# Second product of the feed-forward block as seven products on quarters, in a two-layer hybrid block on one core

## The chip, the cores and the metric

One core of a Trainium2 chip runs the whole program. The metric is device time in microseconds of one execution, the median of several. All arithmetic is fp32: TensorE multiplies a rounded type (fp32r), so a product of two fp32 matrices is made of three matmuls (below).

## What is computed

Two layers over 512 tokens of 1024 numbers, weights of each layer different:

```python
def reference(x, positions, ...):
    for l in range(2):
        h = rms_norm(x, pre_mix_norm[l])
        z = h @ w_in[l]                       # 1024 -> 1932, split in 13
        mix = concat(conv_group(..), pool_group(..), sgu_group(..), nsa_group(..))
        x = x + rms_norm(mix @ w_out[l], post_mix_norm[l])
        h = rms_norm(x, pre_ffn_norm[l])
        f = square(relu(h @ ffn_w1[l]))       # 512x1024 @ 1024x4096
        x = x + rms_norm(f @ ffn_w2[l], post_ffn_norm[l])   # 512x4096 @ 4096x1024
    return x
```

The change is in the last two lines of the loop, the feed-forward block (ffn), and in where some tiles of the four mixers lie.

## The kernel before

**One recorder orders everything.** The program first records every instruction of the five engines in `_Rec.add`, with what it depends on, an assumed duration (`cost`) and a key: its place in the recording plus `shift`. `order` then takes, again and again, the engine that can start an instruction earliest by these assumed durations, and on it the instruction that is ready first, ties by key; tiles of a pool are handed out in recorded order. `issue` writes the result out, so the order on each engine is fixed, and each instruction waits for semaphores only. All instructions come out of `issue`, which is why every row of the profile shows line L442; tiles tell them apart. Transfers go into the assumed time as one stream (L401 to L406): bytes at 360 per ns, then 2 us for one of SyncE and 4 for one of GpSimd.

**Products.** An fp32 operand is split in hi and lo parts: ScalarE copies it, rounding (`wh` of a weight tile `wr`), and VectorE subtracts (`wl`). `mm3` (L473) multiplies hi by hi, hi by lo, lo by hi into one PSUM bank. A weight tile (a unit, 128x1024, 512 KB) is loaded by SyncE into one of six `wr` buffers and split into one of five places for `wh` and `wl`. A sum of weight tiles is made by a transfer on GpSimd's queue that adds another tile of memory to the buffer (`more`).

**First product of the ffn.** The 4096 inner columns are taken in four parts of 1024; each part in two halves `i` of 512. `square4` does a half by seven products on quarters (Winograd's form of Strassen's scheme): the tokens, the inner rows and the columns are halved; the seven left forms (`hF`: A11, A12, A22, S1 to S4) are built from the normed input by `norm_forms` once per layer, and the right ones come from four weight tiles by adding transfers. Its PSUM banks are named `pf`. The results are squared after ReLU and split into the tiles `f` (hi and lo, 512 columns for every row tile of 128 inner columns).

**Second product of the ffn.** It is a plain product, per part 8 row tiles of `f` by 4 token tiles, for each of two halves of 512 output columns: `tgroup` runs over units of two row tiles, with three 512-column matmuls a pair. The left half of the columns goes to `pm` banks and is summed over the parts in `y` (ScalarE copies in part 0, VectorE adds later); the right half keeps four own banks `po` over all parts. In the last part VectorE and ScalarE also make the squares and the products with the gain `gb`, `post` adds to `xres`, and `norm_tile` builds `h` and its transpose `hT` for the next layer, one token tile after another.

**Memory.** Twelve tiles of 8 KB per partition (`big`) hold `hF`, `f`, `y`, mixer outputs and weights ahead; gains lie in a small pool (`grow`), and the mixers' convolution inputs `ch`, `V`, `Vc`, `pch` and `cst` in the pool `mp`.

PSUM has eight banks, three under the tag "mm", one "o", two "s", two "x"; the `po` banks take "x" and "s" for the whole ffn. What this section calls the last first product of a part is the last use of a `pf` bank in it.

## Time and profile before

| | |
|---|---|
| median of 3 runs | 1082.05 us (1081.45 to 1082.11) |
| profiled execution | 1081.48 us, its span 1079.8 us |
| TensorE busy in the span | 1064.2 us (99%) |
| VectorE busy | 726.2 us (67%) |
| ScalarE busy | 505.8 us (47%) |
| GpSimd busy | 92.7 us (9%) |
| granted TensorE clock, mean | 0.998 |

The busy times are shares of one span in which different stages alternate: the mixers, the output product, four ffn parts, twice. A part is 84 us, so the eight parts make 672 us of it. Which engine sets the end of a stage is to be read from that stage: windows show each engine's busy time in a stretch, the chain of waits shows what released what, and the timeline shows single instructions.

### The profile page before, as it was taken

The page shows a single profiled execution, that of the slowest core. Times are in us where ns is not written, and L with a number is a line of the kernel's source. Part 1 is how long each engine was busy: PE and PEld are TensorE (multiplying, and loading weights), DVE is VectorE, ACT ScalarE, POOL GpSimd, SP SyncE. Part 2 cuts the span into 40 slices and gives each one's busy share as a digit, 9 for nine tenths or more (in the row PEclk, how much of TensorE's full clock was granted, in tenths as well). Part 3 has the DMA queues.
Part 4 walks back from the last instruction along what each step waited for, and adds up shares of the span by engine and source line. Part 5 has one row for each costly group of instructions (what it writes and reads, how often), then busy time and mean ns, then how long its engine had stood idle before and what let it go on. Part 6 is the DMA issues. An engine that isn't in the chain of part 4 may idle for free.

```text
span 1079.8 us, 16960 instructions
## 1 busy us (share of the span) xinstructions
PE 1064.2 (99%) x6850; PEld 935.5 (87%) x6850; DVE 726.2 (67%) x1118; ACT 505.8 (47%) x893; POOL 92.7 (9%) x144
## 2 busy tenths in 40 slices
PE   7999999999999999999999999999999999999997
PEld 6998777898898898898899986789989989988986
DVE  7799875895275266267669997769924743752773
ACT  5437774753252253254444487658423523433431
POOL 3000002200100100100000000111000000000000
PEclk9999999999999999999999999999999999999999
DMA  9330216455656566467144111245665655656511
GB/s 341 99 118 21 79 47 159 115 130 183 138 155 175 110 169 175 98 150 230 37 129 136 60 57 42 59 118 119 190 141 112 165 170 120 175 157 137 147 50 78
DMA packets 39265, 137.44 MB, mean 127 GB/s; under 512 B 4753, under 2 KB 5649, under 8 KB 38930
## 3 DMA queue, kind: packets, MB, share of 16 engines
q1 hardware_dynamic: 29970, 102.79, 28.4%
q0 software_dynamic: 9216, 33.56, 18.9%
q8 instruction: 54, 0.88, 0.3%
q14 instruction: 25, 0.20, 0.1%
HBM read 134.23 MB, written 2.10 MB: 126 GB/s over the span
## 4 chain that ended last, share of the span: by engine, by line
PE 88%; DVE 7%; ACT 1%; issue 1%; DMA 1%; POOL 1%; POOLq 0%; DVEq 0%; SPq 0%; ACTq 0%
PE pf L442 30%; PE pm L442 22%; PE po L442 16%; PE pp L442 7%; PE pc L442 4%; PE s L442 2%; PE O L442 2%; PE ppt L442 2%; DVE wl L442 2%; PE pt L442 1%; DVE cacc L442 1%; DVE pw L442 1%; DMA wr<-wst 1%; DVE xb L442 0%; POOL r L442 0%
## 5 line engine op out<-in xcount | busy, mean ns | idle before, releaser
L442 DVE TENSOR_TENSOR wl<-wr,wh 128x1024 fp32r<-128x1024 f32 (+1 forms) x220 | 262.1, 1202 | 178.3 <-ACT wh L442 176.1
L442 ACT ACTIVATE wh<-wr 128x1024 fp32r<-128x1024 f32 (+1 forms) x222 | 227.7, 1042 | 279.3 <-DMA wr<-wst 90.5
L442 PE MATMUL pf<-hF,wh 128*128 128x256 f32 x1728 | 313.4, 283 | 1.1 <-DVE hF L442 0.8
L442 PEld LDWEIGHTS pf<-hF,wh 128*128 128x128 f32 x1728 | 270.4, 192 | 3.1 <-DVE hF L442 1.2
L442 PE MATMUL pf<-hF,wl 128*128 128x256 f32 x864 | 243.4, 283 | 0.0
L442 PEld LDWEIGHTS pf<-hF,wl 128*128 128x128 f32 x864 | 165.4, 192 | 1.2 <-DVE wl L442 0.7
L442 PE MATMUL pm<-wh,f 128*128 128x512 f32 x512 | 161.8, 392 | 0.0
L442 PE MATMUL po<-wh,f 128*128 128x512 f32 x512 | 159.5, 389 | 0.0
L442 PEld LDWEIGHTS pm<-wh,f 128*128 128x128 f32 x512 | 96.2, 188 | 22.4 <-DVE s L442 1.7
L442 PEld LDWEIGHTS po<-wh,f 128*128 128x128 f32 x512 | 96.1, 188 | 19.9
L442 POOL DMA_DIRECT2D wr<-wst x64 | 55.4, 866 | 569.2 <-DVE wl L442 411.5
L442 PE MATMUL pp<-wh,hT 128*128 128x256 f32 (+1 forms) x512 | 101.4, 291 | 0.0
L442 PE MATMUL pm<-wl,f 128*128 128x512 f32 x256 | 100.0, 391 | 0.0
L442 PE MATMUL po<-wl,f 128*128 128x512 f32 x256 | 99.8, 390 | 0.0
L442 DVE SCALAR_TENSOR_TENSOR cacc<-ch,cwh,cacc 128x512 f32<-128x512 f32 x120 | 85.1, 743 | 0.5
L442 PE MATMUL pm<-wh,mixT 128*128 128x512 f32 x256 | 83.3, 401 | 0.1
L442 PEld LDWEIGHTS pp<-wh,hT 128*128 128x128 f32 x512 | 80.9, 190 | 0.6
L442 PE MATMUL pp<-wl,hT 128*128 128x256 f32 (+1 forms) x256 | 74.3, 290 | 0.0
L442 PEld LDWEIGHTS pm<-wh,mixT 128*128 128x128 f32 x256 | 47.7, 188 | 12.0 <-issue 1.0
L442 PEld LDWEIGHTS po<-wl,f 128*128 128x128 f32 x256 | 48.1, 188 | 9.9
L442 PEld LDWEIGHTS pm<-wl,f 128*128 128x128 f32 x256 | 48.2, 188 | 8.8
L442 PE MATMUL pm<-wl,mixT 128*128 128x512 f32 x128 | 50.2, 395 | 0.0
(236 smaller groups left out, 1376.9 us busy)
## 6 DMA issues: line engine op xcount, KB each, us to landing
wr<-wst SPq DMA_DIRECT2D x170, 512.0 KB, 4.3
wr<-wst POOLq DMA_DIRECT2D x64, 512.0 KB, 5.8
gb<-rows SPq DMA_DIRECT2D x7, 512.0 KB, 5.1
wr<-wq SPq DMA_DIRECT2D x8, 268.0 KB, 4.8
xres<-x SPq DMA_DIRECT2D x4, 512.0 KB, 6.1
cw<-cw SPq DMA_DIRECT2D x2, 1024.0 KB, 8.2
out<-xres SPq DMA_DIRECT2D x3, 512.0 KB, 2.6
sgw<-sgw SPq DMA_DIRECT2D x2, 256.0 KB, 5.5
```

The source lines that it names most:

```text
L442: getattr(getattr(nc, e), method)(*[real(x) for x in args], **{k: real(x) for k, x in kw.items()})
```

## The change

**The second product** of each part becomes seven products too. The part's 512 x 1024 inner matrix (the left operand) has quarters A11, A12, A21, A22, where the first index is the half of the tokens and the second the half `i` of the 1024 inner columns. `square4` now hands its four results (`emit`) to `put`, which builds seven left forms in 8 KB tiles: A11 and S3 from the first half, A12, S1, S2, S4 and A22 from the second. Each product is 2 token tiles by 4 row tiles by 3 matmuls of 512 columns. Right operands are two units each: as loaded for p1, p2 and p3, and sums by adding transfers for p5, p6, p7 and q4. The banks of p1 and p7 keep summing over the parts; the other five go through banks of the tags "mm" and "o" and are summed in `acc` (`add_up`). After the last part they are combined into the four quarters of the output, each followed by `done`: squares, the gain, `post` and `norm_tile`.

By the order, over the whole program: TensorE's matmuls fall by 192; splits of a weight tile go from 212 to 260 on VectorE and from 214 to 262 on ScalarE; all rows of VectorE from 1120 to 1288, of ScalarE from 767 to 955; adding transfers from 64 to 128; loads of units from 170 to 186.

**Around it**: two of four results of a first product are squared by ScalarE; the order of the seven first products is another; the norm rows (`gains`) and the small mixer tiles (`rest`) lie in 8 KB tiles, of which there are 14; the planner's assumed cost of an adding transfer changes.

```diff
-NBIG, NSC = 12, 9
+NBIG, NSC = 14, 9
...
-                dma = max(dma, end + 1.1) + v.pn * v.ix.size * 4 / 360e3
-                end = dma + (2.0 if e == "sync" else 4.0)
+                dma = max(dma, end + 1.1) + v.pn * v.ix.size * 4 / (360e3 if e == "sync" else 180e3)
+                end = dma + 2.0
...
+TAGS = "mm", "o"
+FIN = (1, 1), (1, 0)
...
+    def gains(self, *rows):
+
+        t = self.big("gb", F32).rearrange("p a b -> p (a b)")
+        r = self.a["rows"]
+        out = [t[:, i * D:i * D + D] for i in range(2)]
+        for v, (l, c0) in zip(out, rows):
+            self.nc.sync.dma_start(v, bass.AP(tensor=r.tensor, offset=r.offset + l * r.shape[1] + c0,
+                                              ap=[[0, P], [1, D]]))
+        return out
...
         s3, s1 = four("hs"), four("hs")
+        self.tt(s3, r0, pts[0], ALU.subtract)
+        put(5, s3)
         self.act(s1, pts[1])
         self.tt(s1, s1, pts[0], ALU.subtract)
         put(3, s1)
-        self.tt(s3, r0, pts[0], ALU.subtract)
         self.stt(r0, s1, -1.0, r0, ALU.mult, ALU.subtract)
         put(4, r0)
         self.nc.shift = FORM3
-        put(5, s3)
         self.stt(r1, r0, -1.0, r1, ALU.mult, ALU.subtract)
         put(6, r1)
...
-        h = self.mp.tile([P, 30 + S], F32, name=self.nm("ch"), tag="ch", bufs=2)
+        h = self.rest[:, 542 * b:542 * b + 542]
...
+
+    def square4(self, l, u, F, emit, early=None):
...
         def finish(c, op, bh, th):
+            if (bh, th) in FIN:
+                self.act(c, c, AF.Relu, scale=1.0 if op == ALU.max else -1.0)
+                self.act(c, c, AF.Square)
+            else:
+                self.stt(c, c, 0.0, c, op, ALU.mult)
+            emit(bh, th, c)
...
-        more(B11, 2)
         B12 = self.load(l, u + 2)
         more(B12, 3)
+        more(B11, 2)
+        t3 = self.split(B12)
+        y = bank()
+        product(y, t3, S3, True)
         t1 = self.split(B11)
         x = bank()
         product(x, t1, S1, True)
         c = snap("c", x)
-        more(B11, 3)
-        t2 = self.split(B11)
+        add(c, y)
+        more(B12, 0)
+        if early is None:
+            first()
+        t2 = self.split(B12)
         z = bank("o")
         product(z, t2, S2, True)
         add(s1, z)
         add(c, s1)
...
+        accs = [y, self.big("acc", F32), self.big("acc", F32)]
+        acc = {"q4": accs[0][:, 0:2], "p2": accs[0][:, 2:4], "p5": accs[1][:, 0:2], "p6": accs[1][:, 2:4],
+               "p3": accs[2][:, 0:2]}
+
+        own = {"p1": [self.pst([P, 512], "po", "x") for _ in range(2)],
+               "p7": [self.pst([P, 512], "po", "s") for _ in range(2)]}
...
+            def put(name, bh, v):
+                if name not in form:
+                    form[name] = self.big(name)
+                o = slice(2 * bh, 2 * bh + 2)
+                hi = form[name][:, o, :256]
+                self.act(hi, v)
+                self.tt(form[name][:, o, 256:], v, hi.bitcast(F32), ALU.subtract)
+            def emit0(bh, th, v):
+                raw["A21" if th else "A11", bh] = v
+                if not th:
+                    put("A11", bh, v)
+                if ("A11", bh) in raw and ("A21", bh) in raw:
+                    s3 = self.scr("s3").rearrange("p (b q) -> p b q", b=2)
+                    self.tt(s3, raw["A11", bh], raw["A21", bh], ALU.subtract)
+                    put("S3", bh, s3)
+            def emit1(bh, th, v):
+                raw["A22" if th else "A12", bh] = v
+                if not th:
+                    put("A12", bh, v)
+                if ("A12", bh) in raw and ("A22", bh) in raw:
+                    a11, a21, a12, a22 = (raw[n, bh] for n in ("A11", "A21", "A12", "A22"))
+                    self.tt(a21, a22, a21, ALU.subtract)
+                    put("S1", bh, a21)
+                    self.stt(a11, a21, -1.0, a11, ALU.mult, ALU.subtract)
+                    put("S2", bh, a11)
+                    self.stt(a12, a11, -1.0, a12, ALU.mult, ALU.subtract)
+                    put("S4", bh, a12)
+                    put("A22", bh, a22)
...
+            def add_up(name, pss):
+                for i in range(2):
+                    v = acc[name][:, i]
+                    if part == 0:
+                        self.act(v, pss[i])
+                    else:
+                        self.tt(v, pss[i], v, ALU.add)
...
+            def done(t, half, v, sign):
+                junk = self.scr("junk")
+                self.nc.shift = POST
+                self.square(v, ssv[:, t, half:half + 1], junk)
+                self.nc.shift = 0
+                gg = g2[:, 512 * half:512 * half + 512]
+                if sign > 0:
+                    self.tt(v, v, gg, ALU.mult)
+                else:
+                    self.stt(v, v, -1.0, gg, ALU.mult, ALU.mult)
+                half_of[t, half] = v
+                if (t, 0) in half_of and (t, 1) in half_of:
+                    self.post(t, [half_of[t, 0], half_of[t, 1]], ssv[:, t])
+                    if after:
+                        self.norm_tile(t, *after)
...
+            def weights(first, j, *steps):
+                if (first, j) not in raws:
+                    raws[first, j] = self.load(l, uw + first + j)
+                x = raws[first, j]
+                for i in steps:
+                    more(x, uw + i + j)
+                return self.split(x)
+            if end:
+                steps = {"p5": lambda j: weights(0, j, 4), "p6": lambda j: weights(0, j, 6),
+                         "q4": lambda j: weights(0, j, 2), "p7": lambda j: weights(4, j, 6)}
+            else:
+                steps = {"p5": lambda j: weights(0, j, 4), "p7": lambda j: weights(4, j, 6),
+                         "p6": lambda j: weights(4, j, 0), "q4": lambda j: weights(4, j, 2)}
+            simple = lambda i: lambda j: self.split(self.load(l, uw + i + j))
+            steps.update(p1=simple(0), p2=simple(2), p3=simple(6))
+            left = {"p1": "A11", "p7": "S3", "p2": "A12", "p5": "S1", "p6": "S2", "p3": "S4", "q4": "A22"}
+            for name in ["p1", "", "p2", "p5", "p6", "p3", "p7", "q4"] if end else \
+                    ["p1", "", "p7", "p2", "p5", "p6", "p3", "q4"]:
+                if not name:
+                    for _ in sq[1]:
+                        pass
+                    if end:
+                        g2, g0 = self.gains(*[(l, 3072), (l + 1, 0)][:1 + (l + 1 < L)])
+                        if l + 1 < L:
+                            after = g0, self.new_hT()
+                place = {"p2": "p1", "q4": "p7"}.get(name, name) if end else name
+                if place in own:
+                    ps = own[place]
+                    product(ps, steps[name], form[left[name]], part == 0, end and name != place,
+                            end and name == "q4")
+                else:
+                    ps = banks()
+                    product(ps, steps[name], form[left[name]], by_tile=end and name == "p3")
+                    add_up(name, ps)
+                for i in range(2):
+                    y11, y12, y21 = (acc[n][:, i] for n in ("p2", "p3", "q4"))
+                    U, w = acc["p6"][:, i], acc["p5"][:, i]
+                    if name == "p1":
+                        plus(U, ps[i])
+                    elif name == "p2":
+                        plus(y11, ps[i])
+                        done(i, 0, y11, 1)
+                    elif name == "p6":
+                        plus(w, U)
+                        plus(y21, U)
+                    elif name == "p3":
+                        plus(y12, w)
+                        done(i, 1, y12, -1)
+                    elif name == "p7":
+                        plus(w, ps[i])
+                        done(2 + i, 1, w, -1)
+                    elif name == "q4":
+                        plus(y21, ps[i])
+                        done(2 + i, 0, y21, 1)
```

VectorE, end of the ffn of layer 0. The names: `s1` and `c` are first-product results, `acc_391`, `acc_392` and `y_298` the sums over the parts, `pm` and `po` banks of second products, `gb` gains, `xres` the residual, `h` and `hT` the next layer's input, `wl` lo splits. Before, after the last sums in `y`:

```order
L442 TENSOR_TENSOR y_306_2087<-pm_707_5129,y_306_2087 128x512
L442 TENSOR_TENSOR y_306_2087<-y_306_2087,gb_399_2419 128x512
L442 TENSOR_TENSOR wl_741_5228<-wr_739_5078,wh_740_5220 128x1024
L442 TENSOR_TENSOR y_306_2087<-pm_708_5064,y_306_2087 128x512
L442 TENSOR_TENSOR wl_802_5242<-wr_800_5096,wh_801_5231 128x1024
L442 TENSOR_TENSOR y_306_2087<-y_306_2087,gb_399_2419 128x512
L442 TENSOR_SCALAR rs_743_5272<-ssv_400_5184 128x1
L442 TENSOR_TENSOR yg_742_5267<-po_401_3043,gb_399_2419 128x512
L442 SCALAR_TENSOR_TENSOR xres_93<-y_306_2087,r_744_5277,xres_93 128x512
L442 SCALAR_TENSOR_TENSOR xres_93<-yg_742_5267,r_744_5277,xres_93 128x512
```

After, in the same place, behind the second products:

```order
L442 TENSOR_TENSOR acc_391_3079<-po_396_2911,acc_391_3079 128x512
L442 TENSOR_SCALAR rs_829_5540<-ssv_390_5320 128x1
L442 SCALAR_TENSOR_TENSOR h_822_5525<-xres_93,r_825_5538,gb_783_5129 128x512
L442 SCALAR_TENSOR_TENSOR xres_93<-y_298_2069,r_830_5546,xres_93 128x512
L442 SCALAR_TENSOR_TENSOR h_823_5530<-xres_93,r_825_5538,gb_783_5129 128x512
L442 SCALAR_TENSOR_TENSOR acc_392_3117<-acc_392_3117,gb_783_5129 128x512
L442 SCALAR_TENSOR_TENSOR acc_391_3079<-acc_391_3079,gb_783_5129 128x512
L442 SCALAR_TENSOR_TENSOR xres_93<-acc_392_3117,r_830_5546,xres_93 128x512
L442 TENSOR_TENSOR hT_786_5578<-pt_826_5552,hT_784_5565 128x4x128
L442 TENSOR_TENSOR hT_787_5582<-pt_827_5567,hT_785_5576 128x4x128
L442 TENSOR_SCALAR rs_834_5584<-ss_831_5560 128x1
L442 TENSOR_TENSOR wl_849_5586<-wr_801_5100,wh_848_5522 128x1024
```

Between the last lo split of the ffn (wl_741) and the next layer's first input there stood the output's own rows, one token tile at a time; now sums, gains and xres rows of two token tiles at a time stand in front of the next lo split of the ffn (wl_849).

GpSimd, adding transfers in the middle parts of layer 0 (`wr` with a number is one buffer's use by one chain). Before, a part and a half, eight to a part:

```order
L442 DMA wr_516_3051<-wst 128x1024
L442 DMA wr_486_2903<-wst 128x1024 x2
L442 DMA wr_512_2997<-wst 128x1024 x3
L442 DMA wr_574_3657<-wst 128x1024
L442 DMA wr_570_3646<-wst 128x1024
L442 DMA wr_600_3779<-wst 128x1024
L442 DMA wr_570_3646<-wst 128x1024 x2
L442 DMA wr_596_3725<-wst 128x1024 x3
```

After, less than one part, sixteen to a part:

```order
L442 DMA wr_565_3356<-wst 128x1024
L442 DMA wr_568_3416<-wst 128x1024
L442 DMA wr_539_3247<-wst 128x1024
L442 DMA wr_565_3356<-wst 128x1024
L442 DMA wr_568_3416<-wst 128x1024
L442 DMA wr_581_3540<-wst 128x1024
L442 DMA wr_584_3677<-wst 128x1024
L442 DMA wr_565_3356<-wst 128x1024
L442 DMA wr_568_3416<-wst 128x1024
L442 DMA wr_612_3853<-wst 128x1024
L442 DMA wr_608_3797<-wst 128x1024
```

Before, every chain belongs to a first product; now the chains wr_565 and wr_568 of the second product, three links each, stand between those of the first.

TensorE, the last matmuls of the kernel, `wh` and `wl` being the halves of a weight tile. Before:

```order
L442 MATMUL po_1144_8204<-wh_1472_10282,f_1390_10091 128x512
L442 MATMUL po_1144_8204<-wl_1473_10289,f_1390_10091 128x512
L442 MATMUL po_1144_8204<-wh_1472_10282,f_1392_10110 128x512
L442 MATMUL po_1144_8204<-wh_1472_10282,f_1390_10091 128x512
L442 MATMUL po_1144_8204<-wl_1473_10289,f_1390_10091 128x512
L442 MATMUL po_1144_8204<-wh_1472_10282,f_1392_10110 128x512
L442 MATMUL po_1144_8204<-wh_1475_10340,f_1390_10091 128x512
L442 MATMUL po_1144_8204<-wl_1476_10348,f_1390_10091 128x512
L442 MATMUL po_1144_8204<-wh_1475_10340,f_1392_10110 128x512
L442 MATMUL po_1144_8204<-wh_1475_10340,f_1390_10091 128x512
L442 MATMUL po_1144_8204<-wl_1476_10348,f_1390_10091 128x512
L442 MATMUL po_1144_8204<-wh_1475_10340,f_1392_10110 128x512
```

After:

```order
L442 MATMUL po_1224_8261<-wh_1656_10794,A22_1608_10592 128x512
L442 MATMUL po_1224_8261<-wl_1657_10816,A22_1608_10592 128x512
L442 MATMUL po_1224_8261<-wh_1656_10794,A22_1608_10592 128x512 x2
L442 MATMUL po_1224_8261<-wl_1657_10816,A22_1608_10592 128x512
L442 MATMUL po_1224_8261<-wh_1656_10794,A22_1608_10592 128x512
L442 MATMUL po_1224_8261<-wh_1658_10830,A22_1608_10592 128x512
L442 MATMUL po_1223_8246<-wl_1659_10877,A22_1608_10592 128x512
L442 MATMUL po_1223_8246<-wh_1658_10830,A22_1608_10592 128x512 x2
L442 MATMUL po_1223_8246<-wl_1659_10877,A22_1608_10592 128x512
L442 MATMUL po_1223_8246<-wh_1658_10830,A22_1608_10592 128x512
```

Before, the last matmuls belong to one token tile (one bank), with all weights of the half at hand; now two banks alternate by weight tile, and the matmuls behind wl_1659 of both banks are the last ones.

## Rows read from the trace of the kernel before

**Rows 1.** Head of the page: span, busy time, share, instructions of an engine.

```profile
span 1079.8 us, 16960 instructions
...
PE 1064.2 (99%) x6850; PEld 935.5 (87%) x6850; DVE 726.2 (67%) x1118; ACT 505.8 (47%) x893; POOL 92.7 (9%) x144
```

**Rows 2.** Chain that ended last, two middle parts: start, length, what.

```profile
290.26 37.43 PE pf L442 x312
327.70 5.51 PE pm L442 x24
...
352.60 21.76 PE po L442 x96
374.36 37.43 PE pf L442 x312
```

**Rows 3.** Windows: length, busy of PE, PEld, DVE, ACT, POOL, clock, DMA share.

```profile
202.00:243.50 41.50, 40.79 (x333) 39.94 (x333) 40.49 (x59) 26.77 (x42) 6.06 (x7) 1.00 0.65 153
374.36:458.48 84.12, 84.12 (x531) 76.11 (x530) 45.42 (x53) 30.60 (x36) 6.87 (x8) 1.00 0.59 151
458.48:542.60 84.12, 84.11 (x537) 75.90 (x536) 57.67 (x77) 39.06 (x63) 5.49 (x10) 1.00 0.49 135
```

**Rows 4.** Groups by form, TensorE: busy, mean ns, idle before.

```profile
L442 PE MATMUL pt<-ident,h 128*128 128x128 f32 x128 | 20.8, 290 | 2.5 <-DVE h L442 2.1
```

**Rows 5.** Timeline, VectorE, last part of layer 0: start, length, instruction.

```profile
522.36 1.21 DVE L442 TENSOR_TENSOR wl<-wr,wh 128x1024 fp32r<-128x1024 f32 x1
523.49 0.68 DVE L442 TENSOR_TENSOR y<-y,gb 128x512 f32<-128x512 f32 x1
...
539.17 0.21 DVE L442 TENSOR_SCALAR rs<-ssv 128x1 f32<-128x1 f32 x1 [0.68 <-ACT yg L442]
539.30 0.68 DVE L442 TENSOR_TENSOR yg<-po,gb 128x512 f32<-128x512 f32 x1
539.89 0.68 DVE L442 TENSOR_TENSOR hT<-pt,hT 128x512 fp32r<-128x512 f32 x1
540.49 0.74 DVE L442 SCALAR_TENSOR_TENSOR xres<-y,r,xres 128x512 f32<-128x512 f32 x1
541.15 0.75 DVE L442 SCALAR_TENSOR_TENSOR xres<-yg,r,xres 128x512 f32<-128x512 f32 x1
```

**Rows 6.** Timeline, end of the kernel: TensorE, ScalarE, VectorE.

```profile
1072.93 0.39 PE L442 MATMUL po<-wh,f 128*128 128x512 f32 x1
...
1073.36 0.60 ACT L442 ACTIVATE yg<-po 128x512 f32<-128x512 f32 x1 [4.75 <-PE po L442]
...
1075.69 0.75 DVE L442 SCALAR_TENSOR_TENSOR xres<-yg,r,xres 128x512 f32<-128x512 f32 x1
```

**Rows 7.** Timeline, GpSimd and ScalarE: an adding transfer and the split behind it.

```profile
439.86 0.86 POOL L442 DMA_DIRECT2D wr<-wst  x1 [14.14 <-DVE wl L442]
...
445.29 1.06 ACT L442 ACTIVATE wh<-wr 128x1024 fp32r<-128x1024 f32 x1 [7.47 <-DMA wr<-wst]
```

**Rows 8.** DMA view, window 374.36 to 458.48: packets, MB, share; issues.

```profile
q0 software_dynamic: 1154, 4.20, 29.7%
q1 hardware_dynamic: 2304, 8.39, 28.8%
...
wr<-wst SPq DMA_DIRECT2D x16, 512.0 KB, 4.8
wr<-wst POOLq DMA_DIRECT2D x8, 512.0 KB, 5.9
```

**Rows 9.** DMA view, windows 448.8 to 453.2 and 439.5 to 448.

```profile
q0 software_dynamic: 144, 0.52, 74.9%
...
q0 software_dynamic: 288, 1.05, 69.7%
```

**Rows 10.** Windows, columns as in rows 3: a short stretch.

```profile
444.75:445.50 0.75, 0.75 (x5) 0.63 (x4) 0.00 (x0) 0.21 (x1) 0.00 (x0) 1.00 1.13 186
```

More of the change, by code (lines that the diff above doesn't have):

```diff
@@ L1227, in square4 @@
         add(c, s1)
-        more(B11, 1)
-        if early is None:
-            first()
-        t3 = self.split(B12)
-        y = bank()
-        product(y, t3, S3, True)
-        add(c, y)
         finish(c, ALU.min, 1, 1)
+        more(B12, 1)
         w22 = self.split(self.load(l, u + 3))
@@ L1240, in square4 @@
         finish(c, ALU.min, 1, 0)
-        t4 = self.split(B11)
+        t4 = self.split(B12)
         product(y, t4, A22)
@@ new lines, in ffn, with banks, product, plus @@
+        acc = {"q4": accs[0][:, 0:2], "p2": accs[0][:, 2:4], "p5": accs[1][:, 0:2], "p6": accs[1][:, 2:4],
+               "p3": accs[2][:, 0:2]}
+        own = {"p1": [self.pst([P, 512], "po", "x") for _ in range(2)],
+               "p7": [self.pst([P, 512], "po", "s") for _ in range(2)]}
+        u0 = U_FF
+        for part in range(NPART):
+            end = part == NPART - 1
+            uw = u0 + PART
+            form, raw = {}, {}
+            def put(name, bh, v):
[26 more added lines that the diff above has]
+                    put("A22", bh, a22)
+            def banks():
+                return [self.pst([P, 512], "pm", TAGS[i]) for i in range(2)]
+            def product(pss, units, a, first=True, final=True, by_tile=False):
+                ws = {}
+                order = [(u, t) for u in range(2) for t in range(2)]
+                for u, t in sorted(order, key=lambda x: x[::-1]) if by_tile else order:
+                    if u not in ws:
+                        ws[u] = units(u)
+                    wh, wl = ws[u]
+                    c = slice(P * t, P * t + P)
+                    d = slice(256 + P * t, 256 + P * t + P)
+                    for kk in range(2):
+                        k = 2 * u + kk
+                        o = slice(512 * kk, 512 * kk + 512)
+                        self.mm3(pss[t], a[:, k, c], a[:, k, d], wh[:, o], wl[:, o], first and k == 0,
+                                 final and k == 3)
+            def add_up(name, pss):
[5 more added lines that the diff above has]
+                        self.tt(v, pss[i], v, ALU.add)
+            def plus(v, w):
+                self.tt(v, w, v, ALU.add)
+            def done(t, half, v, sign):
[13 more added lines that the diff above has]
+                        self.norm_tile(t, *after)
+            more = lambda x, i: self.nc.gpsimd.dma_start(x, self.a["wst"][l, i], accum_op=ALU.add)
+            sq = [self.square4(l, u0 + 4 * i, F, e, y[:, i] if part == 0 else None)
+                  for i, e in enumerate((emit0, emit1))]
@@ L1377, in ffn @@
-            u0 += n // 2
-            if end and l + 1 < L:
-                after = self.new_norm(l + 1, 0)
-            for t, ps in self.tgroup(lambda j: self.unit(l, u0 + j), srcs, n // 2 if end else 2, own, part == 0, end):
+                    for v in sq:
+                        next(v)
+            for _ in sq[0]:
+                pass
+            half_of = {}
+            raws = {}
+            def weights(first, j, *steps):
[5 more added lines that the diff above has]
+                return self.split(x)
```

62 lines of the change are left out of this document (13 added, 49 removed).

## The prediction

> **What bounds the kernel now.** I read the page's head first: in a span of 1079.8 us TensorE is busy 1064.2 us, 99% [rows 1]. Then the chain of work that ended last: a middle part of the feed-forward block (ffn) is one unbroken run of matmuls on it, 37.43 us of first products (pf), then second products (pm, po), and the next part starts 84.10 us after this one [rows 2]. The windows by stage say the same: in the part at 374.36 us TensorE is busy 84.12 of 84.12 us at granted clock 1.00 (the upper of its levels, 2.4 GHz), VectorE 45.42, ScalarE 30.60 [rows 3]. So time goes with the number of matmuls as long as everything that feeds them stays hidden. Who comes next differs by stage: VectorE has 39 us to spare in a middle part, 26 in a last part (57.67 of 84.12), and one in the 41.5 us before part 0 of layer 0 ends its first products (40.49) [rows 3].
>
> **Prices.** A 512-column matmul: 21.76/96 = 0.2267 us; a 256-column one 37.43/312 = 0.120 [rows 2]. A transpose of h 20.8/128 = 0.16 [rows 4]. VectorE rows from start to next start, back to back: a lo split (wl, 128x1024) 1.13, a 512-column tensor_tensor 0.60, one with a scalar operand per partition 0.66, the tiny rs 0.13 [rows 5].
>
> **Term 1, matmuls removed.** The plain second product of a part is 8 k x 4 t x 3 x 2 halves = 192 matmuls, the seven products are 7 x 24 = 168. 24 x 0.2267 = 5.44 us a part, eight parts: **-43.5 us**. A middle part would take 84.1 - 5.4 = 78.7.
>
> **Term 2, end of layer 0.** This is what I think the change pays with. Before, a last part ran its second product for 46 us with VectorE lightly used: after the last first product 13 VectorE rows, 10 us, stood ahead of wl_741, the last lo split of the ffn. Now forms, seven pairs of sums, products with the norm, and the next layer's input all come after that point. By the order, from the row of VectorE that reads pf_760 (the last first product) to wl_895 stand 75 rows: 40 of 0.60, 14 of 0.66, 13 of 1.13, 8 of 0.13 = 24.0 + 9.2 + 14.7 + 1.0 = 49.0 us. TensorE has, until its first matmul that needs wl_895, 141 x 0.2267 + 16 x 0.16 + 48 x 0.120 = 32.0 + 2.6 + 5.8 = 40.3 us. TensorE thus waits at least 9 us for VectorE, in waits on sums, on hT and on splits. VectorE is not always supplied: followed row by row it stands some 2 us at the first sum of the sixth product's bank (pm_810) and some 4 at pm_804, and enters with about 1 us of arrears; then TensorE loses up to 18. I take **+15** (9 to 18), nearer the walk, because each of those waits is a fixed place in a fixed order.
>
> A rule speaks for more. Rows show that the next VectorE operation starts 0.59 us after one recorded as 0.68 [rows 5]. The Trainium skill, VectorE: DVE Perf Modes, section The DRAIN you can't avoid, says that the next operation does not start until the pipeline is empty; with full recorded durations (0.68, 0.74, 1.22, 0.21) the 75 rows would be an estimated 55 us, 6 more. The trace disagrees for operations that wait for nothing, so the sum goes by the intervals.
>
> **Term 3, end of layer 1.** The same without the next layer: VectorE to wl_1659, the last split, 10 x 1.13 + 35 x 0.60 + 4 x 0.66 + 2 x 0.13 = 35.2 us; with a quarter of a microsecond ahead, a hop of 0.2 and the ten matmuls behind it (2.3) TensorE ends 38.0 us after its last first product, where 141 matmuls alone are 32.0: at least +6, by the walk +9. Behind the last matmul, before: ScalarE 0.43 us after its start, and the last xres ends at 1076.44, 3.1 after the last matmul's end at 1073.32 [rows 6]. Now two row tiles finish together, so four xres rows and two chains through GpSimd instead of one: some 5.3, +2. Together **+10** (6 to 13).
>
> **Term 4, six middle parts.** After the last first product VectorE has 15 rows before the split that the product S2 needs (13 x 0.60 + 2 x 1.13 = 10.1, with a hop and waits some 11.5), while TensorE has 45 matmuls of earlier products, 10.2 us. 0.3 to 1.5 us are left open in each; upper end 2. **+7** (0 to 12). In bulk there is room: per middle part splits go 22 to 28 and 512-column rows 30 to 44, 28 x 1.13 + 44 x 0.60 = 58.0 us of 78.7; ScalarE goes from 36 to 58 operations at 30.60/36 = 0.85 [rows 3], 49 us.
>
> **Term 5, the weights' sums.** Four products take sums of weight tiles, made by transfers that add: 16 instead of 8 a part on GpSimd's queue, ordinary loads 18 instead of 16. A link of such a chain is: issue, 5.43 us to the start of the hi split [rows 7], 1.06 for it, 1.13 for the lo split, then the next transfer into the same tile; 7.6 to 8.5 us. A chain has at most three links, 26 us of a 79 us part, and others run beside it. GpSimd itself: 16 x 0.86 = 14 us [rows 7]. I cost it at 0, with what it hides behind being the six weight tiles in flight (wr); if that cover goes it is the second rival.
>
> **Term 6, rest.** At the ffn's start VectorE's work between the first hF and the last first product of part 0 grows from 53.8 to 56.7 us by the same prices, but TensorE gets 36 second-product matmuls (8.2 us) in that stretch: 0 (-1 to +2). Two of four results of a first product are squared by ScalarE instead of VectorE, counted above. The small mixer tiles only change their place; no instruction is added: 0. The norm rows stay seven loads.
>
> **Sum.** -43.5 + 15 + 10 + 7 = -11.5. The profiled run took 1081.48 us, its span 1079.8, so 1.7 lie around the span and stay; the run is 0.57 below the median 1082.05. 1081.48 - 11.5 = 1070.0, against the median **1070.5**.
>
> **Rivals.** First, VectorE's order bends and TensorE stays full: waits where I counted them are covered by rows done earlier, as with the last parts of before, where 57.67 us of VectorE in 84.12 cost TensorE nothing [rows 3]. Then the terms 2 to 4 vanish and 1082.05 - 43.5 = 1038.6. Against it: 49.0 us of rows against 40.3 of matmuls is a count, not a wait. 12%.
>
> Second, slower: **the 16 DMA engines become the bound** of the middle parts. There, 16 loads take 28.8% of 84.1 us, 1.51 us of all engines each, and 8 adding transfers 29.7%, 3.12 each [rows 8]. After: 18 x 1.51 + 16 x 3.12 = 77.1 us in a part of 78.7, 98%. If the engines can't be kept busier than 94%, a part takes over 82 us and six of them give back 20, which with terms 2 and 3 is the whole gain; that is the point from which it decides. At 90% a part is 85.7, 6 x 7.0 = +42, and -43.5 + 15 + 10 + 42 = +23.5: **1105.5**. For it: six tiles in flight can hardly keep engines that full, and one adding transfer by itself fills only 74.9% of its 4.4 us [rows 9]. Against it: transfer times overlap, since the share in a short window is 1.13 [rows 10] and two at once cost 0.697 x 8.5 / 2 = 2.96 each, where one alone costs 3.30 [rows 9]. The Trainium skill, DMA: Bandwidth & Descriptors, section Issuing engines are not separate DMA queues, says that transfers of every starting engine run on the same 16 engines and interleave, so the queue of GpSimd brings no room of its own; the shares above one show that the sum of packet times still isn't a hard limit. 14%.
>
> Third, the gain is eaten where the counts point, with all terms at their upper ends: -43.5 + 18 + 13 + 12 = -0.5, 1081.5, no change. 12%.
>
> **How the numbers follow.** Main case 62%, rivals 12, 14, 12. A measurement of this kernel tells some 0.2% (2.2 us) from no change. Faster: the first rival and nearly all of the main case, 0.72. Same: most of the third and the upper rim of the main case, 0.12. Slower: the second and the rest, 0.16. Range: below, the lower bounds -43.5 + 9 + 6 - 1 = -29.5, 1053; above, the upper bounds with the start's 2 (1083.5) and the milder half of the second rival, parts of 82.7 us, 1088. The first rival and the harder half of the second are left out, 19%.
>
> **What would show it.** Term 1: po and pm matmuls of the second product 192 fewer, mean interval unchanged. Term 4 and the second rival: distance between the starts of two middle parts 78.7 to 80; 82 and more, with waits of ScalarE's wh on DMA and a share near 1, is the second rival. Terms 2 and 3: in the last parts TensorE busy for 10 to 18 us less than the window, its idle time ended by VectorE's splits, sums or h, VectorE near full. Tail: last xres some 5 us behind the last matmul. I am wrong if the last parts' windows show TensorE full, or the middle parts gaps of over 3 us.

## The result, and the profile after

The changed kernel takes 1091.58 us (median of 4 runs, 1090.35 to 1092.88), the kernel before 1082.04: a ratio of 1.009, interval 1.0072 to 1.0107. It is slower by 9.5 us, where 1070.5 was forecast. The profiled execution took 1092.38 us, its span is 1090.7.

The head of its page (span, busy time and share of each engine; answers to [rows 1]):

```profile
span 1090.7 us, 17187 instructions
...
PE 1043.6 (96%) x6658; PEld 900.7 (83%) x6658; DVE 849.6 (78%) x1286; ACT 628.3 (58%) x1081; POOL 152.5 (14%) x208
```

The matmuls did fall by 192 (6850 to 6658), but TensorE's busy time only by 20.6 us, not by 43.5, and 47 us of the span are now without it, where 16 were. The windows by stage (columns as in [rows 3]: two middle parts of layer 0, its last part up to the next layer's `pp` products, the last part of layer 1, and the tail) say where:

```profile
287.25:367.51 80.26, 79.62 (x504) 70.66 (x503) 58.91 (x71) 46.31 (x60) 13.83 (x16) 1.00 0.91 221
367.51:450.91 83.40, 80.17 (x505) 70.86 (x504) 60.28 (x73) 43.88 (x57) 13.79 (x16) 1.00 0.89 217
450.91:582.30 131.39, 115.80 (x729) 102.68 (x728) 98.45 (x136) 65.50 (x105) 20.03 (x27) 0.94 0.64 166
992.78:1082.00 89.22, 83.35 (x505) 72.66 (x503) 71.42 (x94) 47.03 (x69) 14.06 (x16) 0.96 0.72 172
1082.00:1090.70 8.70, 0.00 (x0) 0.00 (x0) 4.48 (x9) 0.72 (x2) 1.72 (x2) 0.65 0.31 121
```

The middle parts are near what was forecast. The ends aren't, and in them the granted clock of TensorE isn't 1.00 any more (0.94 and 0.96). The same cut for all profiles, in us, by the starts of TensorE's first products (a last part is counted to the next layer's `pp` products, or to the end of the span; "mixers" is from there to the second ffn; the first ffn's late start is left out):

| kernel | three parts, layer 0 | last part, layer 0 | mixers, layer 1 | three parts, layer 1 | last part, layer 1 |
|---|---|---|---|---|---|
| before | 84.3, 84.1, 84.1 | 111.4 | 166.8 | 84.4, 84.1, 84.1 | 90.7 |
| forecast by the terms | 239.7 in all | 120.9 | 166.8 | 239.8 in all | 95.3 |
| after | 80.3, 80.3, 83.4 | 131.4 | 168.2 | 79.9, 81.7, 80.7 | 97.9 |
| last part plain (e1) | 79.8, 80.5, 83.0 | 112.0 | 168.1 | 80.6, 81.1, 80.5 | 91.8 |
| all parts plain (e2) | 84.0, 84.4, 84.4 | 110.4 | 168.3 | 84.0, 84.4, 84.4 | 91.1 |
| no adds (e3) | 79.9, 80.4, 80.1 | 132.4 | 168.4 | 79.9, 80.4, 80.1 | 97.8 |
| waits filled (e4) | 79.9, 80.6, 80.2 | 128.2 | 168.2 | 80.8, 80.5, 81.3 | 96.9 |
| 13 tiles (e5) | 78.9, 81.7, 80.7 | 119.1 | 166.8 | 80.2, 83.2, 80.0 | 96.2 |
| 13 tiles, last part plain (e6) | 78.9, 81.8, 79.3 | 111.5 | 166.7 | 79.4, 82.6, 78.9 | 91.9 |
| fewer VectorE rows (e7) | 79.9, 80.1, 80.1 | 122.3 | 168.1 | 80.7, 82.0, 80.5 | 87.9 |
| old assumed price (e8) | 81.5, 79.4, 82.8 | 118.6 | 168.1 | 84.3, 80.5, 82.9 | 97.4 |
| 13 tiles, S2 late (e9) | 78.9, 81.7, 79.9 | 123.6 | 166.8 | 78.9, 82.6, 79.0 | 95.9 |
| 13 tiles, old price (e10) | 83.3, 84.3, 83.3 | 118.9 | 166.6 | 85.7, 82.6, 81.9 | 96.6 |
| e6 with the old price (e11) | 84.4, 83.7, 81.4 | 112.8 | 167.0 | 84.3, 81.6, 78.9 | 92.1 |

From before to after the last part of layer 0 lost 20.0 us and that of layer 1 7.2, the mixers with the first start of an ffn 2.7, and the six other parts gave back 19.0.

In the last part of layer 0 TensorE's waits are these (who waited for whom, total us, times, longest):

```profile
PE pf L442 <- ACT wh L442: 3.5, 1, 3.5
PE po L442 <- DVE wl L442: 3.4, 2, 2.8
PE po L442 <- DVE acc L442: 2.5, 1, 2.5
PE pt L442 <- DVE h L442: 2.2, 1, 2.2
PE pm L442 <- DVE wl L442: 1.9, 1, 1.9
```

Four of the five are ended by VectorE, as the forecast's second term has it. VectorE in turn waited in the same stretch (its own waits, 500 to 565 us):

```profile
DVE acc L442 <- PE pm L442: 8.1, 3, 4.3
```

So the two take turns. The chain that ended last, in that stretch (start, length, what), shows VectorE on it to 513.86, then TensorE alone for 17 us, then VectorE again:

```profile
510.90 0.34 DVE y L442
...
512.71 1.15 DVE wl L442
513.86 0.04 issue
513.90 9.52 PE pm L442 x33
523.42 4.67 PE po L442 x20
...
529.49 1.18 PE pm L442 x5
530.66 0.02 issue
530.69 0.70 DVE acc L442
```

During those 17 us TensorE, by the order, runs the second weight tile of S2's product last, behind one token tile of S4's product and nearly all of p7's. VectorE needs S2's sums before it can put any token tile together; it splits weights meanwhile and stands idle for 8.1 of the 17 us. Behind 530.7 it has all the rest left. 33 matmuls in 9.52 us are 0.288 each, where 20 in 4.67 are 0.233: the first of them ran at a lower clock.

### The profile page after: what moved, and what is told of

The parts are those of the page before. It is cut to its first block, busy times and chain, and to the rows that moved or that the text cites. A ratio compares the mean times of both kernels' runs of the same rounds, so it can differ in the third digit from the quotient of the medians.

```text
span 1090.7 us, 17187 instructions
## 1 busy us (share of the span) xinstructions
PE 1043.6 (96%) x6658; PEld 900.7 (83%) x6658; DVE 849.6 (78%) x1286; ACT 628.3 (58%) x1081; POOL 152.5 (14%) x208
## 4 chain that ended last, share of the span: by engine, by line
PE 66%; DVE 15%; DMA 10%; ACT 4%; issue 4%; POOL 1%; POOLq 0%; DVEq 0%; SPq 0%; ACTq 0%
PE pf L442 21%; PE pm L442 20%; DMA wr<-wst 9%; PE pp L442 6%; PE po L442 6%; DVE wl L442 4%; PE pc L442 4%; PE O L442 2%; PE s L442 2%; ACT wh L442 2%; PE ppt L442 2%; DVE cacc L442 2%; DVE acc L442 1%; PE pt L442 1%; DVE c L442 1%
## 5 line engine op out<-in xcount | busy, mean ns | idle before, releaser
L442 DVE TENSOR_TENSOR wl<-wr,wh 128x1024 fp32r<-128x1024 f32 (+1 forms) x268 | 318.7, 1204 | 97.0 <-ACT wh L442 96.8
L442 ACT ACTIVATE wh<-wr 128x1024 fp32r<-128x1024 f32 (+1 forms) x270 | 276.6, 1042 | 175.9 <-DMA wr<-wst 81.1
L442 POOL DMA_DIRECT2D wr<-wst x128 | 110.9, 908 | 579.7 <-DVE wl L442 339.0
L442 PE MATMUL pm<-wh,S 128*128 128x512 f32 x384 | 129.2, 408 | 8.0 <-ACT S L442 2.9
L442 PEld LDWEIGHTS pm<-wh,S 128*128 128x128 f32 x384 | 73.4, 191 | 33.8 <-DVE acc L442 5.7
L442 PE MATMUL pm<-wh,mixT 128*128 128x512 f32 x256 | 85.7, 407 | 3.1 <-ACT mixT L442 3.1
L442 DVE SCALAR_TENSOR_TENSOR cacc<-rest,cwh,cacc 128x512 f32<-128x512 f32 x120 | 85.0, 741 | 0.5
L442 PEld LDWEIGHTS pp<-wh,hT 128*128 128x128 f32 x512 | 79.9, 189 | 0.6
L442 PE MATMUL pm<-wl,S 128*128 128x512 f32 x192 | 76.5, 403 | 1.9 <-DVE wl L442 1.9
L442 PE MATMUL po<-wh,A 128*128 128x512 f32 x192 | 67.7, 413 | 5.4 <-DVE acc L442 2.5
L442 PE MATMUL pm<-wh,A 128*128 128x512 f32 x192 | 63.8, 399 | 0.6 <-ACT wh L442 0.4
L442 ACT ACTIVATE c<-c 128x512 f32<-128x512 f32 x64 | 38.9, 625 | 23.2 <-DVE c L442 22.4
L442 PE MATMUL pc<-hT,wh 128*128 128x256 f32 x256 | 48.8, 290 | 0.8 <-ACT hT L442 0.8
```

The costliest lines, as they stand in the source:

```text
L442: getattr(getattr(nc, e), method)(*[real(x) for x in args], **{k: real(x) for k, x in kw.items()})
```

## The experiments

Theories: **A**, the ends pay, because VectorE and TensorE wait for one another in the last parts. **B**, the adding transfers crowd the DMA engines. **C**, the granted clock falls behind TensorE's waits and lengthens the ends further. **D**, the mixers lose by the order that a fourteenth 8 KB tile allows.

**e1, the last part plain.**

```diff
+PLAIN = 3
...
+            if part >= PLAIN:
+                after = self.plain(l, part, u0, F, y, acc, own, ssv)
...
+                for v, x in ((U, p1), (y11, p1), (w, U), (y21, U), (y12, w), (w, p7), (y21, p7)):
+                    self.tt(v, x, v, ALU.add)
```

> The last part of each layer makes its second product plainly, in 192 matmuls, as before the change; the partial sums of the seven products of parts 0 to 2 are put together by 14 VectorE rows during that part's first products. Theory A (the ends of the layers pay: VectorE and TensorE wait for each other over forms, sums and norm): the stretch from the start of the last part to the next layer's pp matmuls falls from 131.4 to about 113 us, layer 1's last part with its tail from 97.9 to about 93, middle parts as they are (80.3 to 83.4): about 1068 us in all. Theory B (adding transfers crowd the DMA engines in the last part): some of the loss stays, since next-layer loads still meet the rest, 1075 or more. If the whole of what it gains is below 8 us, A is wrong.

Measured: 1066.08 us, ratio 0.9856 (0.9839 to 0.9872). The last part of layer 0, as a window:

```profile
450.59:562.58 111.99, 111.44 (x753) 101.34 (x752) 79.13 (x108) 55.58 (x93) 11.33 (x18) 1.00 0.52 147
```

TensorE is busy throughout and the clock stays at its upper level. 19.4 and 6.1 us came back, the middle parts stayed. A stands: what the change gains lies in six parts, what it costs lies in two.

**e2, every part plain, the rest of the change kept** (the same edit with `PLAIN = 0`).

> Every part makes its second product plainly; all the rest of the change stays (order of the first products, two results squared by ScalarE, tiles and gains moved, the planner's price). It tells what that rest costs by itself. If the 1.3 and 1.5 us that the mixers of the changed kernel lost come from the moved tiles and gains: about 1085 us, the start of each ffn again 1.3 to 1.5 us later. If they come from the second product's new order: 1082 and the mixers as before. The rest a gain: below 1080.

Measured: 1084.05 us, ratio 1.0022 (1.0013 to 1.0032). The rest costs some 2.6 us by itself, and the mixers are late as in the changed kernel; no gain is hidden there.

**e3, the second product's adding transfers left out, all orders kept.**

```diff
                 for i in steps:
                     more(x, uw + i + j)
+                    self.nc.left_out.add(len(self.nc.ops) - 1)
...
         for i in seq:
+            if i in self.left_out:
+                continue
```

> The 64 adding transfers of the second product are left out when the program is written (so those four products use a single weight tile in place of a sum); the order on every engine is the one of the changed kernel. Theory B (DMA): the six middle parts fall to 78.7 to 79.5 us each, some 9 to 11 us together, the wait before the last first product of layer 0 (some 5 us) goes, about 1076 us. Theory A (order of VectorE and ScalarE): middle parts lose at most 1 us each, the ends stay as long as they are (131 and 98), 1087 or more.

Measured: 1087.93 us, 3.7 less than the changed kernel. Its last part of layer 0:

```profile
447.16:579.58 132.42, 117.06 (x730) 104.13 (x729) 98.52 (x136) 65.49 (x105) 13.15 (x19) 0.92 0.47 133
```

The middle parts lose 5.3 us together and come to 79.9 to 80.4, not to 78.7; the ends don't get shorter. B is small, and 5.3 is its upper figure: 3.3 of it lie in the third part of layer 0, which takes 80.2 and 80.1 us in e4 and e7 too, with the adds in place. Against those two, whose middle parts make 483.4 and 483.3 us, the adds cost 2.5 us. More follows from this run than was asked. Behind the last first product of layer 0 ScalarE waits for no transfer here (3.3 us in the changed kernel), and that stretch is as long as ever, 81.9 us against 80.2. What costs there is not the arrival of weights. Ahead of it TensorE still waits 2.8 us for a weight tile of a first product; the part on term 2 comes back to that.

**e4, TensorE's waits filled.** In five waits of the last part of layer 0 the matmul before is repeated.

```diff
+FILL = {("wh_781",): 26, ("wl_803",): 8, ("po_396", "A22_780"): 10, ("wl_849",): 11, ("pt_858",): 17}
...
+                    for _ in range(todo.pop(key)):
+                        nc.tensor.matmul(real(out), real(lhs), real(rhs), start=False, stop=False,
+                                         skip_group_check=True)
```

> In five waits of TensorE at the end of layer 0, 72 repeated matmuls are put in (26, 8, 10, 11, 17, sized to the waits of 3.5, 1.9, 2.5, 2.8 and 2.2 us), so that it isn't idle there; the repeated products make the result another one. Theory C (the granted clock falls to half behind each of these waits, 0.77 to 0.91 in those stretches, and that lengthens the end): clock 1.00 there, and the last part of layer 0 some 3 to 5 us shorter, 1087 to 1088. If the waits alone count: the same time within 1 us, or longer by what the added matmuls delay.

Measured: 1086.45 us. Windows of the changed kernel that begin at the end of a wait of TensorE (496.9, 513.9, 541.6, 548.7 and 562.2 us); the third number from the right is the granted clock:

```profile
495.00:500.00 5.00, 3.12 (x13) 2.61 (x14) 3.14 (x5) 4.13 (x7) 0.00 (x0) 0.76 1.06 259
...
513.00:518.00 5.00, 4.10 (x11) 3.25 (x12) 3.75 (x5) 1.12 (x2) 1.71 (x2) 0.67 0.75 134
...
541.00:545.00 4.00, 3.41 (x11) 2.78 (x12) 3.55 (x7) 1.94 (x5) 1.57 (x2) 0.62 0.00 0
...
548.50:551.50 3.00, 2.75 (x9) 2.14 (x10) 2.56 (x4) 0.21 (x1) 0.72 (x3) 0.55 0.32 91
...
562.00:565.50 3.50, 3.22 (x15) 2.70 (x16) 3.46 (x7) 1.20 (x2) 1.40 (x1) 0.56 0.23 21
```

Two of the same places with the waits filled, and the whole last part:

```profile
511.00:515.00 4.00, 3.95 (x17) 3.10 (x17) 4.00 (x6) 1.89 (x2) 1.72 (x2) 1.00 0.85 133
...
546.00:549.00 3.00, 3.00 (x21) 2.64 (x20) 3.00 (x5) 1.72 (x3) 0.00 (x0) 1.00 0.32 72
...
448.03:576.26 128.23, 120.71 (x801) 106.60 (x800) 97.76 (x136) 65.55 (x105) 20.05 (x27) 1.00 0.66 171
```

72 matmuls more, and the stretch is 3.2 us shorter: 1.0 before the last first product and 2.2 behind it. C stands: in the changed kernel the clock falls behind these waits, and the stretch is shorter where it doesn't. The size is less sure than the fall. The two profiles differ by 6.6 us (the medians by 5.1), and another 3.2 of it lie in the third part, which the edit doesn't touch (83.4 and 80.2 us); the changed kernel's 83.4 holds waits on a sum and on hi splits. So a stretch with the same order can move that much between two runs.

**e5, 13 tiles of 8 KB in place of 14** (`NBIG, NSC = 13, 9`).

> The changed kernel with 13 tiles of 8 KB instead of 14, nothing else edited; with 13, the order in the mixers has the last transposes of the convolution (pc from cn) 11 rows earlier on TensorE, as before the change. Theory D (the mixers' 1.3 to 1.9 us per layer come from the order that the fourteenth tile lets the planner take): the wait of 1.55 us on ACT mixT at the output product goes, both mixers 1.4 to 1.9 us shorter, 1088 to 1089 us. If the wait comes from the moved tiles or gains themselves: the mixers as in the changed kernel, 1091.

Measured: 1072.13 us (1068.25 to 1073.87), ratio to before 0.9907 (0.9884 to 0.9929). D is right: of the wait in the mixers, in the changed kernel

```profile
PE pm L442 <- ACT mixT L442: 1.6, 1, 1.6
```

nothing is left, and the mixers have their old length. But 16 us more went than was expected, 12.3 of them at the end of layer 0:

```profile
446.78:565.83 119.05, 109.78 (x730) 97.86 (x729) 97.07 (x135) 63.43 (x104) 20.37 (x26) 0.99 0.71 182
```

VectorE does the same work there (97 us against 98), in another order. With 13 tiles the planner, by the order, takes all but two matmuls of S4's product, and all of p7's, behind S2's; VectorE's wait for sums in `pm` (494 to 560 us) is 1.4 us instead of 8.1, and the clock is 0.99:

```profile
DVE acc L442 <- PE pm L442: 1.4, 3, 0.7
```

**e6, 13 tiles and the last part plain.**

> The last part plain (as in the first experiment) and 13 tiles of 8 KB. Theories A and D together: 1066.1 less 3 us, 1063. If the smaller number of tiles binds in the middle parts (seven forms, seven first forms, sums): 1066 or more, with the middle parts longer than 80 us.

Measured: 1059.0 us (1058.07 to 1062.08), ratio 0.9795 (0.9778 to 0.9812): the fastest version here, 2% under the kernel before, and 4 us less than the two theories together gave. Its six middle parts make 480.9 us against 505.2, so the smaller number of tiles doesn't bind them. Against e5 it is 13.1 us faster: even with the better order the last parts are better off plain.

**e7, 22 rows of VectorE per last part left out.**

```diff
             def plus(v, w):
                 self.tt(v, w, v, ALU.add)
+                self.nc.left_out.add(len(self.nc.ops) - 1)
...
                     self.stt(v, v, -1.0, gg, ALU.mult, ALU.mult)
+                self.nc.left_out.add(len(self.nc.ops) - 1)
```

> The changed kernel with 22 rows of VectorE per layer left out of the last part (the additions that put the quarters together and the products with the gain), the order of all else as it was; so the output is another. 20 of them stand behind the last first product of layer 0, 20 x 0.60 = 12 us. Theory A (VectorE's rows in their fixed order are the end's path): the last part of layer 0 shortens by 8 us or more, that of layer 1 by 5 or more, 1078 us or less. Rival (TensorE's own work, the slower clock and the hops between the engines make the end; VectorE's rows are mostly beside them): less than 4 us in all.

Measured: 1072.27 us. The last parts get 9.1 and 10.0 us shorter, for some 12 us of rows each. The last part of layer 0, ahead of and behind the end of its first products:

```profile
447.55:496.68 49.13, 46.42 (x365) 44.62 (x364) 33.27 (x39) 28.75 (x39) 6.93 (x8) 1.00 0.89 227
496.68:569.89 73.21, 62.74 (x368) 53.16 (x366) 52.47 (x76) 36.30 (x67) 12.21 (x19) 0.98 0.55 146
```

7.0 of the 9.1 us lie behind it, where the changed kernel takes 80.2 at a granted clock of 0.91. VectorE's rows there are on the path, as A says. The 7.0 is not the rows alone: what waited for them, and some of the lower clock, went with them.

**e8, the planner's old assumption for an adding transfer.**

```diff
-                dma = max(dma, end + 1.1) + v.pn * v.ix.size * 4 / (360e3 if e == "sync" else 180e3)
-                end = dma + 2.0
+                dma = max(dma, end + 1.1) + v.pn * v.ix.size * 4 / 360e3
+                end = dma + (2.0 if e == "sync" else 4.0)
```

> The changed kernel with the planner's old assumption for an adding transfer (360 per ns, 4 us behind) instead of 180 per ns and 2 us; only the order of instructions changes. If the new assumption is what keeps the middle parts near 80 us: they go to 82 or more and the kernel to 1096 or more. If the assumed price is of no weight: 1089 to 1093.

Measured: 1084.04 us (1080.68 to 1089.5), 7.5 less than the changed kernel, which neither case had. The middle parts are longer (491.3 against 486.2 us), as the first case said, but the end of layer 0 is 12.8 us shorter. So two edits that change none of the work and only what the planner may choose give the same 119 us there.

**e9, 13 tiles, and S2's second weight tile late again.** The one thing that distinguishes the orders most plainly is put back:

```diff
+                    late = 150 if u and a is form.get("S2") and end and l + 1 < L else 0
...
+                    self.nc.shift = late
```

> The changed kernel with 13 tiles of 8 KB, and in the last part of layer 0 alone the twelve matmuls of the sixth product (S2) on its second weight tile get a later key, so that TensorE takes them behind the first tile of S4's product and all of p7's, as the changed kernel with 14 tiles does; nothing else is edited. Theory A' (the end of layer 0 is long because S2's sums come late, and VectorE's rows for the first two token tiles then stand behind all matmuls): the last part of layer 0 goes from 119.0 to 127 to 132 us, the rest as with 13 tiles, about 1082. Rival (the gain of 13 tiles lies elsewhere: memory, the mixers, transfers): 119 to 121, 1072 to 1074.

Measured: 1076.86 us, 4.7 more than with 13 tiles. The last part of layer 0:

```profile
446.35:569.92 123.57, 110.37 (x729) 98.63 (x728) 97.73 (x137) 64.64 (x105) 19.38 (x27) 0.96 0.66 176
```

It lies between the two cases. Behind the last first product the loss is 6.1 us (69.6 to 75.6 us to the next layer's `pp`), of the 9.3 that separate the changed kernel from e5 there when the matmuls left over are counted off (losses of 21.0 and 11.7 us). Late S2 sums, with what the planner moves behind them, are thus some two thirds of it, and the clock is lower again (0.96 against 0.99) without an edit to it. The remaining third is of other places in the order, and which was not tried. The total expected, 1082, was missed: it took the last part to be some 10 us longer, and it is 4.5 longer, since ahead of the last first product this kernel lost 1.5 us less than e5.

**e10, 13 tiles and the old assumption.**

> The changed kernel with 13 tiles and the planner's old assumption for an adding transfer. The order at the end of layer 0 has S2's product whole ahead of S4's and p7's. Theory A': the last part of layer 0 is 117 to 121 us, as with either edit alone, so 1069 to 1076 in all, and the two edits' gains don't add. If each edit took away a cost of its own at the end: 110 or less.

Measured: 1090.03 us (1083.88 to 1090.43). The end of layer 0 is 118.9 us, as with either edit alone, which A' expected. The total was missed, since the six middle parts are 501.1 us instead of 484.7 (e5).

**e11, e6 with the old assumption.**

> The last part plain, 13 tiles, and the old assumption for an adding transfer. With the ends plain, no order of the sums is left there to go wrong, so only the middle parts can move: 1057 to 1063 if the assumption is of little weight in them, up to 1068 if it lengthens them as it did with 14 tiles (81.5, 79.4, 82.8, 84.3, 80.5, 82.9 us).

Measured: 1068.87 us, and uneven (1063.22 to 1073.48), just above the second case. The plain ends hardly move (112.8, 92.1), the middle parts go from 480.9 to 494.2. The new assumed price, part of the change, is thus worth some 13 (e6 to e11) and 16 us (e5 to e10) in the middle parts with 13 tiles, by one profile each; e11's is the slowest of its four runs, and by the medians its 13 are 10 (1059.0 to 1068.9).

## Why the prediction was wrong, step by step

The sum was -11.5 us, the profiles differ by +10.9. Of the 22.4 between, 10.5 are in the last part of layer 0, 6.6 in the six middle parts, 2.7 in the mixers and at the first ffn's start, 2.6 in the last part of layer 1.

**Term 1 was right.** 192 matmuls went. Two prices moved against each other: a chain's piece of 144 first-product matmuls and one of 12 second-product matmuls in the changed kernel are

```profile
451.07 16.96 PE pf L442 x144
468.03 2.80 PE po L442 x12
```

0.118 and 0.233 us each, against 0.120 and 0.2267 [rows 2]. 336 and 168 of them are 39.6 + 39.2 = 78.8 us, the forecast 78.7. Why a 512-column matmul takes 3% longer was not found; e2, with the plain product's matmuls, has it too.

**Term 2 is the step that failed.** It said that after the last first product the 75 rows of VectorE against 40.3 us of matmuls cost 9 to 18 us, and took 15. The last part of layer 0 lost 25.4 us (20.0 longer, with 5.4 us of matmuls gone). That TensorE would wait there for VectorE was right, as e1 and e7 show; the size was not. Behind the last first product the changed kernel takes 80.2 us to the next layer's `pp` where before took 64.6, less 5.4 for the matmuls gone: a loss of 21.0. With the waits filled it is 18.8. So the walk along the order, whose end was 18, came nearer than the count, and a value between the two was the wrong choice: an order is fixed, and a row-by-row walk along it is worth more than a count. That it came so near is in part luck, since the pieces that the term names make 16 (9 by the count, 6 of waits, 1 of arrears). The walk had VectorE stand some 2 us at pm_810, which is a bank of S4's product, and some 4 at pm_804, one of S2's; the trace has 2.5 and 4.3 there, and 1.3 at a sum before them. The order is what makes the difference: in e5, where S2's sums come early, the loss behind the last first product is 11.7 us, near the count's 9. Two things were not in the term at all. The granted clock fell to its lower level, 1.2 GHz, behind each of the five waits of 1.9 us and more, at a price of some 3.2 us of the stretch (e4). And ahead of the last first product 4.4 us were lost, which no term counted: TensorE waited 3.5 us for a hi split, the split for a transfer that added to a first product's tile.

```profile
485.13 10.56 DMA wr<-wst
```

It landed after 10.6 us, where 5.4 us to the start of the split stood in [rows 7], and over these 10.6 us the DMA engines are full, a share of 1.01:

```profile
485.13:495.69 10.56, 8.29 (x71) 8.08 (x69) 5.12 (x7) 3.25 (x5) 2.64 (x3) 1.00 1.01 292
```

Two gains, issued at 482.9 us, and several weight tiles are loaded beside it. With the second product's adds gone (e3) the wait is still 2.8 us, so it isn't mainly these; whether it is the gains, one of which the change loads later than before, was not tried.

**Term 3 was right in kind**: some 41.3 us from the last first product to the end of the last matmul, where the walk's +9 gave 41. The tail is 9.2 us behind the last matmul instead of 6.5; two token tiles finish together there, each with a chain through GpSimd (answering to [rows 6]):

```profile
1082.24 0.68 DVE L442 TENSOR_TENSOR y<-y,gb 128x512 f32<-128x512 f32 x1
1083.36 0.75 DVE L442 SCALAR_TENSOR_TENSOR xres<-acc,r,xres 128x512 f32<-128x512 f32 x1 [0.44 <-POOL r L442]
...
1085.94 0.75 DVE L442 SCALAR_TENSOR_TENSOR xres<-acc,r,xres 128x512 f32<-128x512 f32 x1 [0.44 <-POOL r L442]
1086.61 0.74 DVE L442 SCALAR_TENSOR_TENSOR xres<-y,r,xres 128x512 f32<-128x512 f32 x1
```

12.6 us of loss against 10 taken and 13 as the upper end; 9.2 of it lie between the last first product and the last matmul, 2.8 in the tail, 0.6 ahead of the last first product. Of the 9.2 the waits that the profile names make 4.5: 2.2 us on ScalarE's hi half of a left form, 1.9 on one of its squares, 0.4 on a lo split. The clock fell twice there too (0.52 in the 3.5 us from 1047.0, 0.53 in the 3.6 us from 1074.4). That was not in the term, so it is in part luck that the walk's number was met.

**Term 4 and term 5, the middle parts.** 13.6 us were lost of the 32.6 to be had, 7 were taken. Without adds the loss is 8.3 (e3), so the size of term 4 stands. Its place doesn't: it named VectorE's lo split for S2's product, and in the middle part shown below TensorE's one named wait is 0.6 us for a hi split of ScalarE. Term 5, costed at 0, is 2.5 to 5.3. Of the second rival the longer landing times came, and the point from which it decides was not reached. The DMA view of one middle part (answering to [rows 8]):

```profile
q0 software_dynamic: 2256, 8.25, 57.5%
q1 hardware_dynamic: 2592, 9.44, 32.8%
...
wr<-wst SPq DMA_DIRECT2D x18, 512.0 KB, 7.0
wr<-wst POOLq DMA_DIRECT2D x16, 512.0 KB, 7.5
```

The engines were kept 91% busy in a part of 80.3 us: an adding transfer took 0.575 x 80.26 / 16 = 2.88 us of all engines, not 3.12, a load 1.46. What grew is the time to land, from 5.9 to 7.5 us for the adds and from 4.8 to 7.0 for the plain loads, which are no part of the sums. The Trainium skill, DMA: Bandwidth & Descriptors, section Issuing engines are not separate DMA queues, says that transfers of all starting engines interleave on the same engines; the plain loads' 2.2 us agree.

**Term 6 was wrong by 2.7 us.** No instruction was added for the moved tiles, but a fourteenth 8 KB tile changed the planner's order in the mixers, and TensorE waits 1.6 us for ScalarE's mixT in each layer. With 13 tiles it doesn't (e5). That a tile more can cost was no case of the forecast.

**The rivals.** The first (TensorE stays full) and the third (nothing changes) didn't come; the slower case was given 0.16, for another cause than the one that came. What the range left out is an end worse than all upper bounds: 18 was called the most that an order could cost, with the clock at its upper level.

## What to carry to other kernels

A scheme that saves matmuls in every part of a loop but needs its results put together at the end should be left off in the last part: there it saves no more than in any other part, and its forms, sums and scalings have nothing to hide behind (1091.6 to 1066.1 us with 14 tiles, 1072.1 to 1059.0 with 13). Where a greedy planner sets the order, a buffer more or another assumed price is an edit in its own right: it moved the same work at the end of layer 0 between 119 and 131 us, so such numbers are to be varied and timed before a change is judged. Where a forecast shows TensorE waiting for some microseconds at a time, the lower clock that may follow belongs in the upper bound.

## What the runs showed of the hardware

In the changed kernel, behind its five waits of TensorE of 1.9 to 3.5 us at the end of layer 0, the granted clock was 0.55 to 0.76 in windows of 3 to 5 us, that is, for part of them at the lower of its two levels (1.2 GHz). Matmuls of 512 columns there took 0.43 us from start to start instead of 0.233:

```profile
515.17 0.63 PE L442 MATMUL pm<-wh,S 128*128 128x512 f32 x1
515.60 0.63 PE L442 MATMUL pm<-wl,S 128*128 128x512 f32 x1
```

In the changed kernel's middle parts of layer 0, with waits of up to 1.8 us, it stayed at 1.00. The length of a wait does not settle it, though. Windows that begin at the end of a wait of 2.7 us in e7 (at the same place as the first of the five), of 2.0 us in e4 and of 1.3 us in a middle part of e1:

```profile
492.70:497.70 5.00, 4.93 (x32) 4.26 (x33) 4.92 (x8) 4.87 (x9) 0.00 (x0) 1.00 1.04 273
...
505.30:509.30 4.00, 3.98 (x16) 3.03 (x17) 4.00 (x7) 4.00 (x7) 0.00 (x0) 1.00 1.01 192
...
428.40:433.40 5.00, 4.58 (x12) 3.38 (x13) 5.00 (x6) 2.02 (x2) 0.86 (x1) 0.66 0.86 163
```

The clock stayed at 1.00 behind the first two and fell behind the third. What decides between them is not shown here. Repeating matmuls during the five waits kept it at 1.00, and the stretch with 72 matmuls more was 3.2 us shorter.
